# Gate rows of the attention on ScalarE's DMA queue, and another spacing of the weight-block sums

## The chip, the cores and the metric

The kernel runs on one core of one Trainium2 chip. A core has five engines that run their own instruction streams: TensorE (PE in the profile, its weight loads PEld), VectorE (DVE), ScalarE (ACT), GpSimd (POOL) and SyncE (SP). DMAs are issued from SP, ACT or POOL and are moved by 16 DMA engines that all issuers share. The metric is the device time of one execution in microseconds; lower is better.

## The reference

One layer of a streaming encoder on 512 positions of width 1024, all in float32:

```python
hn = rmsnorm(h, norm_mix_g)
fq, fk, fv, ff, gq, gf, gi, gg = split(hn @ w_in)
log_f = log_sigmoid(ff + fox_f_bias)              # 8 heads of 64
fox = softmax(q k^T / 8 + F[t] - F[s], causal) v  # F = cumsum(log_f), per head
rec = hgrn2_chunkwise(gq, gf, gi, lb)             # gated linear recurrence, 4 heads, state 128x128
rec = rmsnorm(rec, hgrn_norm_g) * silu(gg)
h += concat(fox, rec) @ w_out
h += cross_attention(rmsnorm(h), rmsnorm(mem))    # 4 heads of 256, 256 memory tokens
h += relu(rmsnorm(h) @ w1)**2 @ w2                # d_ff = 4096
out = rmsnorm(h, final_norm_g)
```

## The kernel before

All matrix products are made in a reduced float32 format, with each operand split into a high and a low part: three matmuls stand for one product. A weight block is loaded by SP into a raw buffer (`wr`), ScalarE copies it to its high part (`wh`, line 178), VectorE subtracts to get the low part (`wl`, line 182). There are two raw buffers for the blocks ahead of the MLP (`a` and `b` halves of each numbered panel: wr16b is the second half of panel 16), so the load of a block waits for the low part of the block two before it.

The order on TensorE is written out by hand; on the other engines a scheduler at build time orders instructions by priority (program order, moved by `ahead(...)`), and every engine then runs its list strictly in that order. Between steps of the recurrence and the attention, `fill.run(us)` puts in pieces of projections, so that TensorE has work while the other engines make the softmax.

The stages are: projections and the linear recurrence (to about 155 us), the forgetting attention (about 155 to 278), output projection, cross attention, then the MLP from about 447 us.

The forgetting attention runs over `pairs`: 4 pairs of heads, p, by 4 query blocks, tb; step n = 4p + tb. A step issues the scores of n (lines 996 and 997), the softmax of n (`fox_softmax`: VectorE takes the bias and the row maximum at line 1007, ScalarE the exponential at 1009, VectorE divides at 1011), the transposes of the probabilities of step n-1 (line 1019), and on POOL the bias of step n+1 (lines 987 and 988). The bias needs the row F of its head on all 128 partitions: the gate row `nF` (128x512, 256 KB), read by a broadcasting DMA from the small DRAM buffer Fd. `fox_rows(p)` (line 852) issues the two rows of a pair; for pair 0 it is called in the recurrence at chunk 2, for the later pairs at the end of step tb = 2 of the pair before. `bi`, `nF`, `pts` (the transposed probabilities) and other tiles share a pool of ten buffers.

The MLP's eight groups of hidden units are each done with seven products of half-size blocks in place of eight (groups 2 to 7 in the up half, all in the down half). For this, sums of blocks of w1 (`wsu`) and w2 (`wsd`) are made in DRAM by DMAs from POOL's queue: for each group a list of eight, four that copy a block (line 427) and four that add a block onto it (line 425, accumulating):

```python
for name, add in (("5", 0), ("7", 0), ("5", 1), ("7", 1), ("6", 0), ("6", 1), ("4", 0), ("4", 1)):
```

Two lists, one of w2 and one of w1, are taken in turn, 112 DMAs of 512 KB in all. When they go out is set by `Presum`. Each projection step reports its modelled TensorE time as credit by `presum.tick`; when the credit reaches `self.next` the next DMA is issued, held back by a dependency on the matmul that reported. PACE gives the distance to the following one by the stretch of credit. A distance of None means that no sum is issued by credit up to the next stretch; there, in the attention, each step n issues one sum by `presum.emit()` (line 1087).

```python
while self.jobs and self.spent >= self.next:
    gap = next(gap for begin, gap in reversed(PACE) if self.next >= begin)
    if gap is None:
        self.next = min(begin for begin, _ in PACE if begin > self.next)
        continue
    self.emit()
    self.next += gap
```

Of the kernel before, what the change touches and what calls it, by code (L numbers as in the profile page):

```python
# [16 lines left out]
P = 128  # L17
# [21 lines left out]
NEG = -3.0e38  # L39
SEVEN = (2, 3, 4, 5, 6, 7)  # L40
RAWS, HB, LOADS = 5, 4, 7
PACE = (25.0, 3.0), (106.0, None), (183.0, 3.1), (306.0, 7.0)


@with_exitstack
def emit(
# [22 lines left out]
    te, ve, ac, gp = nc.tensor, nc.vector, nc.scalar, nc.gpsimd  # L69
# [38 lines left out]
    def t2(name, dt=F32, shape=(S,)):  # L108
        return t2p.tile([P] + list(shape), dt, tag="t2", name=name)
# [172 lines left out]
    class Fill:  # L282
        def __init__(self):
            self.q = deque()
            self.credit = 0.0
# [143 lines left out]
    class Presum:  # L429
        def __init__(self):  # L430
            self.jobs, self.spent, self.next, self.at = deque(), 0.0, PACE[0][0], None

# [12 lines left out]
        def tick(self, us, at):  # L445
            self.spent, self.at = self.spent + us, at
# [5 lines that stand above are left out]
# [176 lines left out]
    for hp in range(2):  # L628
        wt = next_panel()
        for j in range(2):  # L630
            h = 2 * hp + j
# [64 lines left out]
    for hp in range(2):  # L696
# [8 lines left out]
        for j in range(2):  # L705
            h = 2 * hp + j
# [6 lines left out]
    Fd = drp.tile([FH, S], F32, name="Fd")  # L713
# [43 lines left out]
    for li, m in enumerate(mlev):  # L757
# [18 lines left out]
        for hp, ps in enumerate(lvs):  # L776
# [18 lines left out]
            for j in range(2):  # L795
                h = 2 * hp + j
# [53 lines left out]
    fF = {}  # L850

    def fox_rows(p):
        for h in (2 * p, 2 * p + 1):
            fF[h] = t2(f"nF{h}")
            gp.dma_start(fF[h], Fd[h, :].partition_broadcast(P))

    mt = []

# [35 lines left out]
    for c in range(NT):  # L894
# [38 lines left out]
        if c == NF:  # L933
            fox_rows(0)
# [122 lines left out]
    for n in range(len(pairs) + 2):  # L1057
# [25 lines left out]
        if n < len(pairs):  # L1083
            fox_scores(*pairs[n])
            if n + 1 < len(pairs):
                fox_biases(n + 1)
            dma = presum.emit()
            if dma is not None:
                tc.keep_in_program_order(dma)
            if tb == 2 and p < 3:  # L1090
                fox_rows(p + 1)
# [606 lines left out]
```

## Time and profile before

| | us |
|---|---|
| median of 3 runs | 764.89 (763.89 to 765.5) |
| profiled execution | 766.35 |
| its span | 764.6 |
| TensorE busy in the span | 749.8 |
| VectorE busy | 538.7 |
| ScalarE busy | 429.9 |
| POOL busy | 228.9 |

The span runs from the first to the last instruction; the profiled execution's own time has 1.75 us around it. Busy times are those of the engines' own instructions. In a timeline a line reads: start, duration, engine, source line, operation, what is written from what is read, shapes, how many were merged, and in brackets the idle time before it and what ended that.

### The profile page before, as it was taken

The page shows a single profiled execution, that of the slowest core. Times are in us where ns is not written, and L with a number is a line of the kernel's source. Part 1 is how long each engine was busy: PE and PEld are TensorE (multiplying, and loading weights), DVE is VectorE, ACT ScalarE, POOL GpSimd, SP SyncE. Part 2 cuts the span into 40 slices and gives each one's busy share as a digit, 9 for nine tenths or more (in the row PEclk, how much of TensorE's full clock was granted, in tenths as well). Part 3 has the DMA queues.
Part 4 walks back from the last instruction along what each step waited for, and adds up shares of the span by engine and source line. Part 5 has one row for each costly group of instructions (what it writes and reads, how often), then busy time and mean ns, then how long its engine had stood idle before and what let it go on. Part 6 is the DMA issues. An engine that isn't in the chain of part 4 may idle for free.

```text
span 764.6 us, 12052 instructions
## 1 busy us (share of the span) xinstructions
PE 749.8 (98%) x4501; PEld 651.7 (85%) x4501; DVE 538.7 (70%) x844; ACT 429.9 (56%) x715; POOL 228.9 (30%) x330
## 2 busy tenths in 40 slices
PE   9999999999997999999999999999999999999996
PEld 6888888888886988888888888898999999998985
DVE  5648773677876657646555558887878797969697
ACT  5654565555754543325443367557575757574773
POOL 7228554444553417841121211101011111000014
PEclk9999999999999999999999999999999999999998
DMA  8689899775878799997497959697969887947342
GB/s 248 193 239 202 194 232 213 184 167 146 214 236 191 215 227 239 228 265 166 141 187 183 260 141 259 210 305 218 307 222 262 250 267 260 272 143 257 129 138 110
DMA packets 99068, 162.86 MB, mean 213 GB/s; under 512 B 6481, under 2 KB 67450, under 8 KB 98562
## 3 DMA queue, kind: packets, MB, share of 16 engines
q0 software_dynamic: 28608, 66.61, 40.2%
q1 hardware_dynamic: 69810, 94.43, 37.5%
q10 hardware_dynamic: 592, 1.05, 0.4%
q8 instruction: 35, 0.57, 0.3%
q14 instruction: 23, 0.19, 0.1%
HBM read 157.87 MB, written 62.93 MB: 289 GB/s over the span
## 4 chain that ended last, share of the span: by engine, by line
PE 88%; DVE 4%; ACT 2%; DMA 2%; issue 2%; POOL 1%; POOLq 0%; ACTq 0%; DVEq 0%; SPq 0%
PE U L1503 4%; PE U L1504 4%; PE U L1505 4%; PE uU L1378 3%; PE uU L1377 3%; PE uU L1376 3%; PE xq L243 2%; PE wo L243 2%; PE xq L244 2%; PE xw L243 2%; PE xq L245 2%; PE xw L245 2%; PE xw L244 2%; PE wo L245 2%; PE u L245 2%; PE u L243 2%
## 5 line engine op out<-in xcount | busy, mean ns | idle before, releaser
L182 DVE TENSOR_TENSOR wld<-wrd,whd 128x1024 fp32r<-128x1024 f32 x56 | 68.5, 1224 | 20.0 <-ACT whd L178 20.0
L178 ACT ACTIVATE whd<-wrd 128x1024 fp32r<-128x1024 f32 x56 | 59.1, 1056 | 26.3 <-PE U L1505 6.5
L425 POOL DMA_DIRECT2D wsd<-in_w_dram x32 | 34.5, 1077 | 112.1 <-PE U L1505 27.4
L178 ACT ACTIVATE whu<-wru 128x1024 fp32r<-128x1024 f32 x42 | 44.4, 1056 | 36.9 <-PE uU L1377 15.4
L182 DVE TENSOR_TENSOR wlu<-wru,whu 128x1024 fp32r<-128x1024 f32 x42 | 50.4, 1222 | 13.3 <-ACT whu L178 13.3
L1503 PE MATMUL U<-whd,hb 128*128 128x512 f32 x120 | 46.8, 390 | 0.0
L1504 PE MATMUL U<-wld,hb 128*128 128x512 f32 x120 | 46.8, 390 | 0.0
L1505 PE MATMUL U<-whd,hb 128*128 128x512 f32 x120 | 46.7, 389 | 0.0
L425 POOL DMA_DIRECT2D wsu<-in_w_dram x24 | 28.5, 1188 | 50.0 <-PE xq L245 8.8
L987 POOL TENSOR_SCALAR bi<-nF,Ft 128x128 f32<-128x128 f32 (+3 forms) x32 | 21.6, 681 | 49.3 <-PE pt L1019 20.8
L1599 POOL TENSOR_TENSOR fa<-acc,gfin 128x512 f32<-128x512 f32 x4 | 6.5, 1656 | 87.6 <-DVE acc L1469 85.2
L427 POOL DMA_DIRECT2D wsd<-in_w_dram x16 | 10.9, 680 | 55.4 <-PE gq L245 13.8
L1378 PE MATMUL uU<-x_hi,wlu 128*128 128x256 f32 x96 | 27.2, 283 | 0.0
L1376 PE MATMUL uY<-xs_hi,whu 128*128 128x256 f32 x96 | 27.2, 283 | 0.0
L1377 PE MATMUL uY<-xs_lo,whu 128*128 128x256 f32 x96 | 27.2, 283 | 0.0
L1378 PE MATMUL uY<-xs_hi,wlu 128*128 128x256 f32 x96 | 27.2, 283 | 0.0
L1376 PE MATMUL uU<-xs_hi,whu 128*128 128x256 f32 x96 | 27.2, 283 | 0.0
L1377 PE MATMUL uU<-xs_lo,whu 128*128 128x256 f32 x96 | 27.2, 283 | 0.0
L1378 PE MATMUL uU<-xs_hi,wlu 128*128 128x256 f32 x96 | 27.2, 283 | 0.0
L1377 PE MATMUL uU<-x_lo,whu 128*128 128x256 f32 x96 | 27.2, 283 | 0.0
L1376 PE MATMUL uU<-x_hi,whu 128*128 128x256 f32 x96 | 27.1, 283 | 0.0
L1133 ACT ACTIVATE x_hi<-hT,gv 128x512 fp32r<-128x512 f32 x16 | 11.5, 716 | 27.5 <-DVE hT L1132 27.5
(997 smaller groups left out, 2695.7 us busy)
## 6 DMA issues: line engine op xcount, KB each, us to landing
wsd<-in_w_dram POOLq DMA_DIRECT2D x48, 512.0 KB, 7.0
wsu<-in_w_dram POOLq DMA_DIRECT2D x36, 512.0 KB, 7.3
wrd<-wsd SPq DMA_DIRECT2D x32, 512.0 KB, 6.3
wrd<-in_w_dram SPq DMA_DIRECT2D x24, 512.0 KB, 5.5
wru<-wsu SPq DMA_DIRECT2D x24, 512.0 KB, 4.5
wru<-in_w_dram SPq DMA_DIRECT2D x18, 512.0 KB, 4.9
wsd<-wsd POOLq DMA_DIRECT2D x16, 512.0 KB, 5.4
wsu<-wsu POOLq DMA_DIRECT2D x12, 512.0 KB, 4.2
```

Of the source, the lines that this page charges most:

```text
L178: ac.activation(hi, raw, AF.Copy)
L182: ve.tensor_tensor(lo, raw, f(hi), ALU.subtract)
L243: te.matmul(ps, wh, hi, start=n_ == 0 and not begun, stop=False)
L244: te.matmul(ps, wh, lo, start=False, stop=False)
L245: at = te.matmul(ps, wl, hi, start=False, stop=k == order[-1])
L425: yield gp.dma_start(dst, block(g, b), accum_op=ALU.add)
L1376: te.matmul(ps[:, i, :], whi[:, k, ws], xh[:, k, :], start=begin, stop=False, skip_group_check=True)
L1377: te.matmul(ps[:, i, :], whi[:, k, ws], xl[:, k, :], start=False, stop=False, skip_group_check=True)
L1378: at = te.matmul(ps[:, i, :], wlo[:, k, ws], xh[:, k, :], start=False, stop=k == UK - 1, skip_group_check=True)
L1503: te.matmul(ps, hi, whi[:, k, :], start=begin, stop=False, skip_group_check=True)
L1504: te.matmul(ps, hi, wlo[:, k, :], start=False, stop=False, skip_group_check=True)
L1505: at = te.matmul(ps, lo, whi[:, k, :], start=False, stop=k == 1, skip_group_check=True)
```

## The change

The two gate rows of each pair are loaded through ScalarE's DMA queue instead of POOL's, and the distances in PACE are altered: 4.0 in place of 3.0 ahead of the attention, 3.0 in place of 3.1 from credit 183, and 6.0 in place of 7.0 from 306. The number of sums per step of the attention is not touched.

```diff
-PACE = (25.0, 3.0), (106.0, None), (183.0, 3.1), (306.0, 7.0)
+PACE = (25.0, 4.0), (106.0, None), (183.0, 3.0), (306.0, 6.0)
...
     def fox_rows(p):
         for h in (2 * p, 2 * p + 1):
             fF[h] = t2(f"nF{h}")
-            gp.dma_start(fF[h], Fd[h, :].partition_broadcast(P))
+            ac.dma_start(fF[h], Fd[h, :].partition_broadcast(P))
```

## The prediction

> **What bounds the kernel now.** I read the page first, then who waited for whom on TensorE, then the timeline of all engines around each wait, and the DMA landings last.
>
> ```profile
> PE 749.8 (98%) x4501; PEld 651.7 (85%) x4501; DVE 538.7 (70%) x844; ACT 429.9 (56%) x715; POOL 228.9 (30%) x330
> ```
>
> TensorE is busy for 749.8 us of a span of 764.6. No change that leaves its matmuls alone can win more than the rest, about 15 us, and most of that is the start and the last normalisation. The waits of TensorE inside the kernel:
>
> ```profile
> PE pt L1019 <- DVE dn L1010: 4.0, 1, 4.0
> PE warm L355 <- DVE ones L359: 1.3, 1, 1.3
> PE gg L271 <- DVE z L671: 1.2, 1, 1.2
> PE pst L906 <- DVE rec L927: 1.1, 1, 1.1
> PE pt L1019 <- DVE bi L1011: 0.7, 1, 0.7
> ```
>
> One wait stands out: a transpose of attention probabilities, 4.0 us. I call the attention's sixteen steps n = 0 to 15 (head pair p = n div 4, query block n mod 4), and T(n) the transposes of step n's probabilities. This wait is ahead of T(11). In the timeline of TensorE:
>
> ```profile
> 241.51 0.28 PE L245 MATMUL xk<-meh,wl18b 128*128 128x256 f32 x1
> 245.80 0.44 PE L1019 MATMUL pt<-ident,bi 128*128 128x128 f32 x1 [4.01 <-DVE dn L1010]
> ```
>
> It costs more than its length, since the granted clock (the third column from the right, behind the engines' busy times) is halved behind it:
>
> ```profile
> 246.00:248.00 2.00, 2.00 (x11) 2.00 (x11) 1.94 (x3) 1.48 (x2) 0.99 (x1) 0.50 1.07 187
> 248.00:250.00 2.00, 2.00 (x11) 2.00 (x11) 1.56 (x9) 0.88 (x4) 2.00 (x5) 0.50 0.94 298
> 250.00:252.00 2.00, 2.00 (x13) 2.00 (x13) 0.51 (x3) 0.34 (x1) 0.52 (x1) 0.58 0.93 240
> ```
>
> Lost there: 2 x 0.50 + 2 x 0.50 + 2 x 0.42 = 2.8 us. The place is worth 4.0 + 2.8 = 6.8 us, by far the largest thing that this change can touch. Why does it wait? VectorE had the maximum of step 11 early, but ScalarE came to the exponential late:
>
> ```profile
> 237.92 0.68 DVE L1007 CUSTOM_DVE_ANT_0 bi<-ps,bi 128x512 f32<-128x512 f32 x1
> ```
>
> ```profile
> 236.18 0.47 ACT L1023 ACTIVATE pts<-pt 128x384 f32<-128x384 f32 x1
> 241.68 1.06 ACT L178 ACTIVATE wh19a<-wr19a 128x1024 fp32r<-128x1024 f32 x1 [5.02 <-DMA wr19a<-in_w_xkv_dram]
> 242.64 0.71 ACT L1009 ACTIVATE bi<-bi,mx 128x512 f32<-128x512 f32 x1
> ...
> 244.63 0.72 ACT L1009 ACTIVATE bi<-bi,mx 128x512 f32<-128x512 f32 x1 [0.71 <-DVE mx L1007]
> ```
>
> In ScalarE's order the split of the weight block wr19a stands ahead of step 11's exponentials, and it sat 5.02 us for the load. From its start (241.68) to T(11) (245.80) are 4.1 us. So the end is set by the landing of wr19a:
>
> ```profile
> 232.46 0.37 SPq L198 DMA_DIRECT2D wr19a<-in_w_xkv_dram  x1
> ```
>
> ```profile
> nF<-Fd POOLq DMA_DIRECT2D x2, 256.0 KB, 9.4
> wr19a<-in_w_xkv_dram SPq DMA_DIRECT2D x1, 512.0 KB, 9.2
> ```
>
> Issued at 232.46, landed 9.2 us later, while on POOL's queue two sums of weight blocks (accumulating, L425) and the gate rows nF of pair 3 were under way:
>
> ```profile
> 230.70 1.16 POOL L425 DMA_DIRECT2D wsu<-in_w_dram  x1
> 231.36 1.67 POOL L855 DMA_DIRECT2D nF<-Fd  x2
> 240.92 0.36 POOL L987 TENSOR_SCALAR bi<-nF,Ft 128x128 f32<-128x128 f32 x1 [7.89 <-DMA nF<-Fd]
> ```
>
> POOL itself waited 7.89 us for those rows, with the next sum queued behind the waiting bias. TensorE did not: step 12's bias was ready before TensorE came out of its own wait.
>
> **The gate rows on ScalarE's queue.** POOL loses eight issues, ScalarE gains eight. Prices, from the only transfers of this size that ScalarE issues and from the rows now:
>
> ```profile
> L1579 ACTq DMA_DIRECT2D out_dram<-fo x4: 338/364/383, 755.0 to 760.7; - x4
> ```
>
> ```profile
> L855 POOL DMA_DIRECT2D nF<-Fd x8: 548/608/1106, 146.2 to 231.9; - x8
> ```
>
> POOL is relieved of 8 x 0.61 = 4.9 us, worth nothing by itself, since none of TensorE's waits above ends on POOL. ScalarE pays 2 x 0.36 = 0.73 us per pair. An issue also waits, in ScalarE's order, for its buffer; the buffer is that of the pair before, free once POOL has made the last bias of that pair, and the exponentials and weight splits would queue behind it. Where the pairs fall, ScalarE sits idle:
>
> ```profile
> 147.07 1.06 ACT L178 ACTIVATE wh11b<-wr11b 128x1024 fp32r<-128x1024 f32 x1 [1.35 <-PE pk L244]
> ```
>
> ```profile
> 207.40 0.60 ACT L961 ACTIVATE xvh<-xv 128x512 fp32r<-128x512 f32 x1 [0.76 <-PE xv L273]
> ```
>
> 1.35 us beside pair 0's issue and 0.76 beside pair 2's, and by the 5.02 us above there is room at pair 3. I take 0, with 0.7 us as upper bound if a pair falls outside such a gap on the way to the 0.7 us wait of T(0).
>
> The transfers themselves: now nF stands behind the sum in POOL's queue, and wr19a shares the engines with one other queue. After the change nF has a queue of its own, all three run at once, and the share of wr19a shrinks until nF is through. The bound comes from the rate of the time when these transfers end:
>
> ```profile
> 237.00:241.00 4.00, 4.00 (x27) 3.61 (x26) 1.61 (x4) 0.00 (x0) 0.08 (x1) 1.00 0.98 331
> ```
>
> The pair is 2 x 256 KB, 0.52 MB, at 331 GB/s 1.6 us. At most all of it goes ahead of wr19a (+1.6 us for T(11)), at least none of it does (0). As nF and wr19a landed within a microsecond of each other (231.4 + 9.4 and 232.46 + 9.2), nearly all of nF now yields to the weight load, and I take +1.5. nF itself should land sooner than 9.4 us; nobody on the path waits for that.
>
> [...]
>
> **The spacing of the sums.** The credit (modelled TensorE time) at which sums go out is read from the code. Before: from 25 every 3.0 up to 106, 27 sums; 16 in the attention, one a step; 40 from 183 at 3.1; 29 from 307 at 7.0. After: from 25 every 4.0, 21 sums; the same 16; 41 from 183 at 3.0; 34 from 306 at 6.0. Ahead of the attention POOL issues six fewer; TensorE's two waits there, 1.2 and 1.1 us, end on VectorE behind chains through several engines. I take 0 for that, with a gain of up to 1 as bound.
>
> In the attention the number is the same, but the sequence is six sums further back. It has copies (L427, 5c 7c, 6c, 4c) and accumulating sums (L425) in turn for two groups. Before, steps 0, 3, 4, 9, 10, 11, 12 and 15 accumulate; after, 0, 1, 2, 5, 6, 9, 10 and 15. So at T(11)'s place (steps 9 and 10) nothing becomes lighter, and step 5 and 6 go from copies to accumulating sums, beside pair 2's rows. What that means, the landings at 199.9 and 204.8 (copies) against those at 225.6 and 230.7 (accumulating):
>
> ```profile
> DMA to landing us min/median/max: 4.8/5.9/6.9
> ```
>
> ```profile
> DMA to landing us min/median/max: 8.1/8.6/9.1
> ```
>
> The weight block then in flight is wr16b. Its split is ahead of step 7's exponentials, as wr19a's is ahead of step 11's:
>
> ```profile
> 203.12 0.37 SPq L198 DMA_DIRECT2D wr16b<-in_w_xkv_dram  x1
> ```
>
> ```profile
> 207.89 1.05 ACT L178 ACTIVATE wh16b<-wr16b 128x1024 fp32r<-128x1024 f32 x1
> ```
>
> ```profile
> 215.86 1.03 PE L1019 MATMUL pt<-ident,bi 128*128 128x128 f32 x8
> ```
>
> If wr16b takes as long as wr19a did, it lands at 212.3, and 4.1 us on, at 216.4, T(7) can start: 0.5 us late. At the lower end it still lands by 211.7 and costs 0. At the upper end it loses another 2.2 us, by which the slowest landing of the accumulating sums exceeds that of the copies (9.1 less 6.9): 2.7 us late. I take 0.5, from the nearest row.
>
> Behind the attention the sums are five or six places late, and denser in the MLP. First and last sum of before in that stretch, and the first fetch of stored sums for the last MLP group:
>
> ```profile
> 442.03 0.71 POOL L427 DMA_DIRECT2D wsu<-in_w_dram  x1 [2.74 <-PE u L245]
> ...
> 656.00 1.05 POOL L425 DMA_DIRECT2D wsd<-in_w_dram  x1 [6.16 <-PE U L1505]
> ```
>
> ```profile
> 683.14 5.73 SPq L1304 DMA_DIRECT2D wru<-wsu  x2
> ```
>
> Credit 307 to 503 took 214 us, 1.09 us a unit. The last sum that group 7's up half needs goes from credit 391 to 408, about 552 us, and is fetched after 683; the very last moves by one unit. No load comes ahead of its sum. Denser sums (one in 6.5 us for one in 7.6) meet a TensorE that is never idle there:
>
> ```profile
> 520.00:600.00 80.00, 80.00 (x520) 73.41 (x519) 65.29 (x80) 52.91 (x72) 9.09 (x10) 1.00 0.85 250
> ```
>
> I take 0: weight blocks are split several ahead of use, and 0.85 of the DMA time leaves room. Without that cover one late block costs what wr19a's does.
>
> **The sum.** 1.5 (T(11)) + 0.5 (T(7)) + 0 + 0 = +2.0 us. The profiled execution took 766.35, 1.75 us around its span of 764.6; it would come to 768.4. The median of the runs shown, 764.89, lies 1.46 below it; on that scale the forecast is 766.9. Its own range is 765.5 to 769.5, from the bounds above.
>
> **The rivals.** *T(11)'s wait goes (faster).* One mechanism: wr19a's split no longer holds up step 11's exponentials. It decides at a landing by 237.6 us (4.1 ahead of 241.7), or at an order on ScalarE with the exponentials first. For it: POOL's queue is rid of 0.52 MB just there, ScalarE's order is laid out anew around the new issues, and the split isn't needed by TensorE for many microseconds. Against: the same bytes are in flight at the same time, with equally heavy sums. Full price -6.8 us, 758.1; where the load is only a few microseconds earlier, 759 to 763. Chance 0.37.
>
> *Nothing on the path moves.* Rows, sums and weight loads share the engines as before, only who issues differs; 764.9, within a microsecond and a half. For it: none of TensorE's waits ends on POOL or on nF. Chance 0.13. [...]
>
> *A second wait of T(11)'s size.* The issues and the shifted sums put another block's split late ahead of exponentials, long enough to halve the clock: +6.8, 771.7. For it: 5.02 us waits for a load do occur; against: only one such in sixteen steps. Chance 0.15.
>
> **How the numbers follow.** Forecast 0.35, of it all slower; with the second wait slower is 0.50. Faster 0.37, same 0.13. A measurement here tells about 0.2% (1.5 us). Cases of both signs are nearly as likely, so the range runs from the full gain to the second wait, 758.0 to 772.0, leaving out a tenth on either side.
>
> **What would show it.** Right: T(11) still waits 4 to 6 us on wr19a's split, the clock halved behind it; nF lands in well under 9.4 us; T(7) waits up to a microsecond; accumulating sums at steps 5 and 6. Wrong: no idle time ahead of T(11), or a wait at a step not named here, or ScalarE waiting at the new issues themselves.

## The result and the profile after

The changed kernel takes 764.3 us (median of 20 executions, 761.13 to 766.92) beside 765.63 for the kernel before on the same chip (763.89 to 767.77). The ratio is 0.9981, interval 0.9972 to 0.9991. In a second measurement it was 762.9 beside 765.07, ratio 0.9969 (0.9955 to 0.9984). So it is faster by 0.2 to 0.3%, 1.3 to 2.2 us. The forecast was 766.9, slower: the time lies in the range, the sign is wrong. A ratio is formed from the executions of both kernels and need not be the quotient of their medians. Two executions are left out of the medians and ratios below as slow: one of 1244.83 us, whose granted clock was 0.557, and one of 770.91.

The profiled execution took 761.13 with a span of 759.4. It is the shortest of its 20, so its span, 5.2 us below that of before, shows the change at its best and not what it mostly does. The first row of its page and the waits of TensorE:

```profile
PE 747.1 (98%) x4501; PEld 649.1 (85%) x4501; DVE 533.4 (70%) x844; ACT 429.9 (57%) x715; POOL 227.0 (30%) x322
```

```profile
PE pt L1019 <- DVE dn L1010: 3.1, 1, 3.1
PE pst L906 <- DVE rec L927: 1.5, 1, 1.5
PE warm L355 <- DVE ones L359: 1.3, 1, 1.3
```

The rows of `gg` (1.2) and of `pt <- DVE bi` (0.7, ahead of T(0)) are gone. The wait at T(11) is still there, a microsecond shorter. TensorE's timeline has T(7) and T(11):

```profile
214.52 1.03 PE L1019 MATMUL pt<-ident,bi 128*128 128x128 f32 x8
243.50 1.22 PE L1019 MATMUL pt<-ident,bi 128*128 128x128 f32 x8 [3.05 <-DVE dn L1010]
```

T(7) has no bracket, so it waited for nothing. Behind T(11) the granted clock (third column from the right) stays at full speed, where before it was halved:

```profile
244.00:246.00 2.00, 2.00 (x19) 1.94 (x18) 1.94 (x3) 1.06 (x2) 1.65 (x2) 1.00 0.16 54
246.00:248.00 2.00, 2.00 (x19) 2.00 (x19) 1.52 (x9) 1.26 (x5) 1.36 (x4) 1.00 0.47 154
```

This adds up: 1.2 + 0.7 + (4.0 - 3.05) + 2.8 of clock, less 0.4 that `pst` waits longer, is 5.3 us of the 5.2. On ScalarE and SP around both places:

```profile
209.68 1.06 ACT L178 ACTIVATE wh16b<-wr16b 128x1024 fp32r<-128x1024 f32 x1 [2.95 <-DMA wr16b<-in_w_xkv_dram]
...
229.12 0.33 ACTq L855 DMA_DIRECT2D nF<-Fd  x1
229.83 0.33 ACTq L855 DMA_DIRECT2D nF<-Fd  x1
...
239.37 1.06 ACT L178 ACTIVATE wh19a<-wr19a 128x1024 fp32r<-128x1024 f32 x1 [4.46 <-DMA wr19a<-in_w_xkv_dram]
```

```profile
231.12 0.37 SPq L198 DMA_DIRECT2D wr19a<-in_w_xkv_dram  x1
```

```profile
nF<-Fd ACTq DMA_DIRECT2D x2, 256.0 KB, 4.9
wr19a<-in_w_xkv_dram SPq DMA_DIRECT2D x1, 512.0 KB, 8.2
```

The gate rows are issued at 229.1, 2.2 us earlier than before (231.36), and land in 4.9 us instead of 9.4. The load of wr19a is issued 1.34 us earlier, because the whole program is that far ahead, and takes 8.2 us instead of 9.2. That last microsecond is the one by which T(11) waits less. Seen from the load, the rows go out 2.0 us ahead of it, where before they went out 1.1 ahead.

### The profile page after: what moved, and what is told of

Read it like the earlier page. It is cut to its first block, busy times and chain, and to the rows that moved or that the text cites. A ratio compares the mean times of both kernels' runs of the same rounds, so it can differ in the third digit from the quotient of the medians.

```text
span 759.4 us, 12056 instructions
## 1 busy us (share of the span) xinstructions
PE 747.1 (98%) x4501; PEld 649.1 (85%) x4501; DVE 533.4 (70%) x844; ACT 429.9 (57%) x715; POOL 227.0 (30%) x322
## 4 chain that ended last, share of the span: by engine, by line
PE 95%; DMA 2%; DVE 1%; ACT 1%; issue 1%; POOL 0%; ACTq 0%; SPq 0%
PE U L1504 4%; PE U L1503 4%; PE U L1505 4%; PE uU L1378 3%; PE uU L1377 3%; PE uU L1376 3%; PE xq L243 2%; PE wo L243 2%; PE xq L244 2%; PE xq L245 2%; PE xw L245 2%; PE xw L244 2%; PE xw L243 2%; PE u L245 2%; PE wo L244 2%; PE u L244 2%
## 5 line engine op out<-in xcount | busy, mean ns | idle before, releaser
L425 POOL DMA_DIRECT2D wsd<-in_w_dram x32 | 34.7, 1084 | 104.0 <-PE uU L1378 22.1
L425 POOL DMA_DIRECT2D wsu<-in_w_dram x24 | 28.5, 1186 | 53.9 <-PE xq L245 8.7
L427 POOL DMA_DIRECT2D wsd<-in_w_dram x16 | 10.9, 680 | 56.8 <-PE gq L245 14.5
```

The source lines that it names most:

```text
L425: yield gp.dma_start(dst, block(g, b), accum_op=ALU.add)
```

## The experiments

The theory after the result: a weight block that lands late, with its split ahead of exponentials in ScalarE's order, is the only wait in the attention that counts, and the DMAs in flight beside it set how late it is. Rivals: the order on ScalarE alone is to blame; the load's own queue sets its time; the new queue, or the new spacing, is enough by itself. Every kernel was timed against the kernel before on its chip, in executions that took turns with it.

### Each part alone, and the split moved

**Queue alone.**

```diff
-            gp.dma_start(fF[h], Fd[h, :].partition_broadcast(P))
+            ac.dma_start(fF[h], Fd[h, :].partition_broadcast(P))
```

> The gate rows on ScalarE's queue, the sums spaced as before. Theory Q (the gain is the rows': wr19a lands sooner once nF has left POOL's queue, 8.2 us for 9.2): T(11) waits about 3 us for 4.0, faster by 1 us, by up to 4 where the clock is not halved. Theory S (the gain is the sums', ahead of the attention): no difference, within 1 us, and T(11) waits 4 us as before. By the prediction on record, slower by 1.5.

Measured 765.08, ratio 0.9999 (0.9987 to 1.0011): no difference. In the profile the rows land sooner, wr19a a little, T(11) waits a little less, and the waits ahead of the attention stay:

```profile
245.76 1.39 PE L1019 MATMUL pt<-ident,bi 128*128 128x128 f32 x8 [3.73 <-DVE dn L1010]
```

```profile
nF<-Fd ACTq DMA_DIRECT2D x2, 256.0 KB, 5.2
wr19a<-in_w_xkv_dram SPq DMA_DIRECT2D x1, 512.0 KB, 8.8
```

**Spacing alone.**

```diff
-PACE = (25.0, 3.0), (106.0, None), (183.0, 3.1), (306.0, 7.0)
+PACE = (25.0, 4.0), (106.0, None), (183.0, 3.0), (306.0, 6.0)
```

> The other spacing of the sums, the gate rows on POOL's queue as before. Theory Q: no difference or, by heavier sums beside pair 2's rows, slower by up to 1 us. Theory S: the waits of 1.2 us (gg) and 0.7 us (T(0)) are gone, faster by 1 to 2 us, and T(11) still waits 4 us. By the prediction on record, slower by 0.5.

Measured 765.12, ratio 0.9993 (0.9982 to 1.0005): nothing that can be told from none. In its profile the waits on `gg` and at T(0) are gone, as in the changed kernel, but T(11) waits as long as before:

```profile
243.47 1.94 PE L1019 MATMUL pt<-ident,bi 128*128 128x128 f32 x8 [4.13 <-DVE dn L1010]
```

**The split of panel 19 behind step 11's exponentials** (kernel before). `len(stream) == 20` holds for panel 19 alone, since panels count from 0.

```diff
-                ac.activation(hi, raw, AF.Copy)
+                at = ac.activation(hi, raw, AF.Copy)
+                if pin:
+                    tc.keep_in_program_order(at)
...
-                    split()
+                    split(pin=len(stream) == 20)
```

> The kernel before, with the split of weight block 19 pinned on ScalarE behind step 11's exponentials. If T(11)'s wait is only the order on ScalarE and is worth 4.0 us and the halved clock 2.8 us, it is gone and the time falls by 4 to 6.8 us. Rival: the late block 19 is wanted next, another wait takes its place, and the time falls by less than 2 us.

Measured 765.01, ratio 1.0 (0.9983 to 1.0017). T(11) waits no more, but two steps on the next late block stands ahead of T(13)'s work. From ScalarE's and TensorE's timelines (source lines are two higher here):

```profile
252.29 1.06 ACT L178 ACTIVATE wh20b<-wr20b 128x1024 fp32r<-128x1024 f32 x1 [1.92 <-DMA wr20b<-in_w_xkv_dram]
```

```profile
256.72 1.09 PE L1021 MATMUL pt<-ident,bi 128*128 128x128 f32 x4 [3.56 <-DVE bi L1013]
```

So the order at this one place is not the cause: with it changed, the next late load is passed on in the same way.

**The changed kernel again**, on this chip.

> The changed kernel once more, to see another of its executions: its times spread over 761 to 767 us and the profiled one was the shortest. Theory: the spread is T(11)'s wait being shorter or longer than what halves the clock; an execution of 763 to 766 us then shows a wait of 3.5 us or more with a clock of 0.50 behind it. Rival: the difference lies spread over the other stages and T(11) waits 3 us at full clock again.

Measured 762.9, ratio 0.9969 (0.9955 to 0.9984). Its profile, an execution of 763.6, is more typical than the first: T(11) waits 3.6 us, and the clock drops for a while (0.89 over 240 to 255 us, where the first profile has 1.00).

```profile
243.41 1.79 PE L1019 MATMUL pt<-ident,bi 128*128 128x128 f32 x8 [3.63 <-DVE dn L1010]
```

### The sums beside the late load taken away

**Two sums less, kernel before.** No sum is lost; the sequence goes on two places later.

```diff
-            dma = presum.emit()
+            dma = None if n in (9, 10) else presum.emit()
```

> The kernel before, without the sums of steps 9 and 10 (they follow later). Theory (contention: wr19a is late because two heavy sums are in flight with it): wr19a lands in 4 to 6 us after its issue instead of 8.6 to 9.2; T(11) waits under 1 us instead of 3.7 to 4.0, its clock is not lowered, the profiled span is 5 to 7 us shorter, and the median falls to 759 to 761. Rival 1 (the wait only moves to the next late block, as when panel 19's split was put behind): T(11) does not wait, but one of T(12) to T(14) does, for 2 to 4 us, and the median stays within 0.2% of 765. Rival 2 (the load's own queue sets its time): it still lands in 8 to 9 us and nothing changes.

Measured 764.51, ratio 0.999 (0.9971 to 1.0009). wr19a landed in 4.6 us and T(11)'s wait was gone, as the theory had it. But the time did not follow, as the first rival had it; the wait came back at T(15), a step later than that rival named. POOL, SP, ScalarE and TensorE, in this order:

```profile
250.19 1.06 POOL L425 DMA_DIRECT2D wsd<-in_w_dram  x1 [0.36 <-issue]
256.09 1.17 POOL L425 DMA_DIRECT2D wsu<-in_w_dram  x1
```

```profile
258.18 0.37 SPq L198 DMA_DIRECT2D wr22b<-in_w_out_dram  x1
```

```profile
266.91 1.06 ACT L178 ACTIVATE wh22b<-wr22b 128x1024 fp32r<-128x1024 f32 x1 [3.94 <-DMA wr22b<-in_w_out_dram]
```

```profile
270.44 0.63 PE L1019 MATMUL pt<-ident,bi 128*128 128x128 f32 x4 [2.60 <-DVE bi L1011]
```

Two accumulating sums (L425) at steps 13 and 14 are now beside wr22b, which is ready 8.7 us after its issue, and T(15) waits. The profiled execution took 761.1, 3.4 us less than the median, so what the slower executions do is not seen here.

**Two sums less, changed kernel.** The same edit.

> The changed kernel, without the sums of steps 9 and 10 (they follow later). Theory (contention): of the changed kernel's waits the 3.1 to 3.6 us ahead of T(11) goes; the time falls from 763 to 764 by 3 to 5 us, to 758.5 to 760.5. Rival 1 (the wait moves on): a wait of 2 to 4 us at one of T(12) to T(14), median 762 to 764. Rival 2 (the load's own queue): landing 8 us, median 762 to 764.

Measured 759.66, ratio 0.9927 (0.9903 to 0.995). Here the theory is borne out in time as well. T(11) on TensorE has no wait:

```profile
239.53 1.04 PE L1019 MATMUL pt<-ident,bi 128*128 128x128 f32 x8
```

No other wait came in the attention. 1.7 us of waits appeared in the first MLP group.

**21 sums at the old spacing** (kernel before).

```diff
-PACE = (25.0, 3.0), (106.0, None), (183.0, 3.1), (306.0, 7.0)
+PACE = (43.0, 3.0), (106.0, None), (183.0, 3.1), (306.0, 7.0)
```

> The kernel before with 21 sums ahead of the attention, as in the changed kernel, but at the old spacing of 3.0 from credit 43 on. Theory (the spacing is what takes away the waits ahead of the attention): the wait of 1.2 us on gg's chain between 75 and 100 us stays (TensorE busy 23.8 to 23.9 of 25 there), the 0.7 us ahead of T(0) may stay or go, and the median is 765 as before. Rival (the number of sums, and with it which of them fall into the attention, is what counts): both waits go as with the new spacing, and the median is that of the new spacing alone, 764.5 to 765.

Measured 765.43, ratio 1.0005 (0.9986 to 1.0023). Neither reading of the waits was right in full. TensorE's busy time (second number) shows the wait on `gg` nearly gone although the sums there are as dense as before, and the 0.7 us ahead of T(0) still there:

```profile
75.00:100.00 25.00, 24.78 (x189) 19.75 (x188) 20.40 (x50) 14.69 (x28) 18.47 (x24) 1.00 0.96 224
150.00:200.00 50.00, 49.31 (x325) 43.24 (x324) 37.41 (x91) 32.64 (x77) 22.86 (x43) 1.00 0.69 167
```

**All splits of panels 12 to 23 in program order** (changed kernel): the edit of panel 19, with `12 < len(stream) <= 24`. These reach back into the attention's first half (in the kernel before, the first of them begins at 162.0 us), further than the expectation says.

> The changed kernel, with all splits of the panels of the attention's second half kept on ScalarE in the order of their place in the program (behind the exponentials of the step). Theory (the order alone is to blame for T(11)'s wait): no wait over 1 us in the attention, profiled span 4 us shorter, median 759 to 761. Rival (the loads are late, and whichever split stands ahead of the exponentials passes it on): when panel 19 alone was put behind, the wait came back as 3.56 us at T(13); with all of them behind it comes back at the products of the late panels themselves, 1 to 4 us in 240 to 275, and the median stays within 0.3% of the changed kernel's.

Measured 775.53, ratio 1.0127 (1.0092 to 1.0163), a loss that neither reading gave in size. The splits come so late that products wait for them, and T(6) and T(7) wait too, 2.61 and 2.04 us:

```profile
209.54 1.18 PE L1021 MATMUL pt<-ident,bi 128*128 128x128 f32 x6 [2.61 <-DVE dn L1012]
...
248.15 0.39 PE L245 MATMUL xk<-meh,wh18a 128*128 128x256 f32 x1 [1.90 <-ACT wh18a L178]
```

### Which part counts once T(11) is clear

All kernels from here on leave out the sums of steps 9 and 10, unless it says otherwise.

**New spacing, rows on GpSimd's queue.**

> The new spacing, gate rows on GpSimd's queue as before, and no sums at steps 9 and 10. Theory (late weight blocks are what counts, and both spacing and the two sums bring them earlier; the queue of the gate rows matters little once the sums are gone): no wait at T(11), profiled span 758 to 759.5, median 759.5 to 761. Rival (the two parts of the change only work together: with the rows on GpSimd's queue the gain stays away, as it did for the spacing alone): median 763.5 to 765.

Measured 759.26, ratio 0.9925 (0.9911 to 0.9939): as fast as with both parts. The place where the kernel before without the two sums waited (POOL, SP, ScalarE):

```profile
249.14 0.67 POOL L427 DMA_DIRECT2D wsd<-in_w_dram  x1
254.84 0.71 POOL L427 DMA_DIRECT2D wsu<-in_w_dram  x1
```

```profile
256.27 0.37 SPq L198 DMA_DIRECT2D wr22b<-in_w_out_dram  x1
```

```profile
262.05 1.06 ACT L178 ACTIVATE wh22b<-wr22b 128x1024 fp32r<-128x1024 f32 x1 [0.39 <-DMA wr22b<-in_w_out_dram]
```

Steps 13 and 14 issue copies (L427) here, since the sequence stands six places further back, and wr22b is ready 5.8 us after its issue.

**New queue, old spacing.**

> The gate rows on ScalarE's queue, the old spacing, and no sums at steps 9 and 10. Theory (spacing counts: the old one leaves the waits of 1.2 and 0.7 us ahead of the attention, and other sums in its last steps): no wait at T(11), waits on gg's chain and at T(0) as before, median 761.5 to 764. Rival (the queue is what counts once T(11) has no wait): median 759.5 to 761.5.

Measured 763.9, ratio 0.9983 (0.996 to 1.0005), executions from 759.01 to 769.38. Steps 13 and 14 accumulate again, and T(15) waits again, with the clock at 0.50 from 274 to 276 us:

```profile
272.13 0.63 PE L1019 MATMUL pt<-ident,bi 128*128 128x128 f32 x4 [3.13 <-DVE bi L1011]
```

**One sum less** (changed kernel, step 10 only).

```diff
-            dma = presum.emit()
+            dma = None if n == 10 else presum.emit()
```

> The changed kernel without the sum of step 10 alone. Theory (the wait is as long as the bytes in flight make wr19a late): wr19a lands between 4.6 us (two sums left out) and 8.2 to 8.8 us (none), at 6 to 7; T(11) waits 0.5 to 2 us with the clock not lowered, median 760 to 762, between 759.7 and 763.5. Rival (only the sum whose transfer covers wr19a's issue counts, that of step 10, issued half a microsecond ahead of it): as with two sums left out, landing under 5 us and no wait.

Measured 764.44, ratio 0.9984 (0.996 to 1.0008). For wr19a the rival was right: it landed in 4.7 us with only the sum of step 10 gone. The time was neither's. Later blocks were late in this execution, and the same chain of split, activation and product passed it on. That sums issued ahead of wr27b and wr35b made them late is argued from the attention, not shown.

```profile
315.56 1.06 ACT L178 ACTIVATE wh27b<-wr27b 128x1024 fp32r<-128x1024 f32 x1 [3.51 <-DMA wr27b<-in_w_xq_dram]
...
437.34 1.06 ACT L178 ACTIVATE wh35b<-wr35b 128x1024 fp32r<-128x1024 f32 x1 [5.96 <-DMA wr35b<-in_w_dram]
```

```profile
320.04 0.50 PE L244 MATMUL xq<-x_lo,wh26b 128*128 128x512 f32 x1 [1.20 <-DVE x_lo L1134]
...
439.06 0.50 PE L243 MATMUL u<-x_hi,wh34b 128*128 128x512 f32 x1 [2.06 <-ACT x_hi L1133]
```

**The two sums made up for behind the attention** (changed kernel).

```diff
-PACE = (25.0, 4.0), (106.0, None), (183.0, 3.0), (306.0, 6.0)
+PACE = (25.0, 4.0), (106.0, None), (183.0, 2.8), (306.0, 6.0)
```

> The changed kernel without the sums of steps 9 and 10, which are made up for by a spacing of 2.8 for 3.0 from credit 183 on. A try at the faster version. Theory (the sums' place behind the attention costs nothing): same as with the two left out and not made up for, 759 to 760.5. Rival (the 1.7 us of waits between 480 and 500 us, in the first MLP group's second half, come from sums that are two places late): they go, 757.5 to 758.5.

Measured 761.77, ratio 0.9955 (0.9936 to 0.9975): by the medians 2 us more than without, though the intervals overlap. Neither reading gave this. The waits in the first MLP group shrank to 0.2 us, and others came at the cross attention's projection, 1.44 and 1.33 us:

```profile
319.81 0.49 PE L243 MATMUL xq<-x_hi,wh26b 128*128 128x512 f32 x1 [1.44 <-ACT x_hi L1133]
```

**New spacing behind the attention alone.**

```diff
-PACE = (25.0, 3.0), (106.0, None), (183.0, 3.1), (306.0, 7.0)
+PACE = (25.0, 3.0), (106.0, None), (183.0, 3.0), (306.0, 6.0)
```

> The kernel before without the sums of steps 9 and 10, with the new spacing behind the attention alone (3.0 and 6.0; ahead of it 3.0 as before). Theory (the gain comes from the part ahead of the attention): waits of 1.2 us on gg's chain and 0.7 us at T(0) as before, a wait at T(15) on panel 22's split, median 763.5 to 765. Rival (the gain comes from the closer sums behind): 759 to 760.5.

Measured 766.28, ratio 0.9999 (0.9978 to 1.0019): nothing. T(15) waits, and here the clock drops behind it:

```profile
270.55 1.09 PE L1019 MATMUL pt<-ident,bi 128*128 128x128 f32 x4 [2.66 <-DVE bi L1011]
```

```profile
270.00:272.00 2.00, 1.45 (x7) 1.48 (x8) 1.86 (x4) 0.71 (x2) 0.00 (x0) 0.64 0.78 264
272.00:274.00 2.00, 2.00 (x11) 1.90 (x9) 0.37 (x1) 0.00 (x0) 0.14 (x1) 0.51 0.84 250
```

**The number of sums alone**: 21 ahead of the attention at the old spacing, the new spacing behind.

```diff
-PACE = (25.0, 3.0), (106.0, None), (183.0, 3.1), (306.0, 7.0)
+PACE = (43.0, 3.0), (106.0, None), (183.0, 3.0), (306.0, 6.0)
```

> Without the sums of steps 9 and 10; ahead of the attention 21 sums as in the changed kernel, but at the old spacing of 3.0 from credit 43 on; the new spacing behind. Theory (the number counts: it sets which sums stand in the attention's steps and so which weight block is late): no wait at T(15), median 759 to 761, with the 0.7 us at T(0) perhaps left. Rival (the wider spacing counts, as it leaves DMA time to the loads ahead): 763 to 765, with a wait at T(15) or a new one in 75 to 200 us.

Measured 759.61, ratio 0.9918 (0.9896 to 0.994): the whole gain, without the wider spacing. The 0.7 us at T(0) stayed. No wait at T(15); ScalarE stood 0.16 us ahead of the split of wr22b, and for an exponential, not the load.

```profile
262.40 1.06 ACT L178 ACTIVATE wh22b<-wr22b 128x1024 fp32r<-128x1024 f32 x1 [0.16 <-ACT bi L1009]
```

**24 sums at a spacing of 3.5**, the new spacing behind.

```diff
-PACE = (25.0, 3.0), (106.0, None), (183.0, 3.1), (306.0, 7.0)
+PACE = (25.0, 3.5), (106.0, None), (183.0, 3.0), (306.0, 6.0)
```

> Without the sums of steps 9 and 10; ahead of the attention a spacing of 3.5 from credit 25 on, 24 sums; the new spacing behind. Theory (the number counts by the place of each sum): another block is late somewhere, with a wait of 2 to 4 us, median 761 to 764. Rival (less is simply better): between the 764.5 of 27 sums and the 759.3 of 21, with no wait in the attention, median 760 to 762 and waits of 0.3 to 1 us ahead of it.

Measured 766.38, ratio 1.002 (0.9996 to 1.0044): fewer sums than before, and yet nothing gained; both readings had given a shorter time. Other sums accumulate beside another block. POOL, then ScalarE:

```profile
258.08 1.09 POOL L425 DMA_DIRECT2D wsd<-in_w_dram  x1
260.30 1.17 POOL L425 DMA_DIRECT2D wsu<-in_w_dram  x1 [1.13 <-PE xk L245]
```

```profile
271.12 1.06 ACT L178 ACTIVATE wh23a<-wr23a 128x1024 fp32r<-128x1024 f32 x1 [4.95 <-DMA wr23a<-in_w_out_dram]
```

TensorE then waited 1.34 and 0.94 us for products of the attention (`pv`), with the clock at 0.96 over 255 to 300 us, and the wait on `gg` grew to 2.0 us. So fewer is not simply better. That the place of each sum in the sequence counts fits all of these runs, but no run moved one sum and left the rest where they were.

### The eight corners

Median in us and ratio to the kernel before on the same chip:

| | all sums | sums of steps 9 and 10 later |
|---|---|---|
| neither part | 765.07 | 764.51, 0.999 (0.9971 to 1.0009) |
| queue | 765.08, 0.9999 (0.9987 to 1.0011) | 763.9, 0.9983 (0.996 to 1.0005) |
| spacing | 765.12, 0.9993 (0.9982 to 1.0005) | 759.26, 0.9925 (0.9911 to 0.9939) |
| both (the change) | 762.9, 0.9969 (0.9955 to 0.9984) | 759.66, 0.9927 (0.9903 to 0.995) |

In three kernels the profile shows TensorE waiting for no late block, neither in the attention nor at the cross attention behind it: spacing, both, and the number alone, each with the two sums later. They are the fastest. Their executions, six each, lie within 1.3, 3.4 and 1.5 us, where those of the other kernels, mostly twice as many, spread over 3.5 to 10.4. They beat both kernels; the simplest of them leaves the rows on GpSimd's queue.

## Why the prediction was wrong

**The term for T(11) had the wrong sign.** The step "I take +1.5", by which a third busy queue holds wr19a up, failed: it was the author's estimate, and no run shows it. The load did not get slower: 8.2, 8.8 and 8.8 us with the rows on ScalarE's queue, 9.2, 9.3 and 9.8 with them on GpSimd's (profiles of the two kernels, of each part alone, of the repeat and of the later start; 8.6 where the split was moved). T(11) waited 3.05, 3.73 and 3.63 us against 4.01, 4.13 and 4.61. Beside the profile of before, the wait gave -1.0, -0.3 and -0.4 us in place of +1.5. The lowered clock behind it had cost 2.8 us before; it cost nothing in the first profile of the changed kernel and 15 x 0.11 = 1.7 us in the repeat (0.89 over 240 to 255 us).

Why the load did not get slower is only in part known. The prediction took all three queues to run at once, and so they did: the rows were under way from 229.1 to about 234, the load from 231.1. What it had not worked out is when ScalarE would issue the rows. They go out beside POOL's sum (229.12 and 229.83, the sum 229.35) and no longer behind it, with a lead of 2.0 us on the load (1.1 before). It also took wr19a to be the one that pays. What took longer was the sum issued with the rows: 9.5 us in the changed kernel, 9.1 before. No run changes the lead alone, so this stays an argument.

**The term for the sums ahead of the attention was too small.** The prediction gave 0 with a gain of up to 1. The waits on `gg` (1.2) and at T(0) (0.7) went in all three profiles of kernels with the new spacing and all sums. Beside the profile of before, `pst` gave back up to 0.4, which leaves 1.5 to 1.9 us, above the stated bound. But `pst` waited 1.1 us in that profile and only 0.2 to 0.7 in the five others with 27 sums ahead of the attention; beside these the gain is 0.6 to 1.5. The failed step was to put these waits down to chains of engines, and not to ask what the sums do to them. That the DMA load is their cause is not shown. Its share at 50 to 75 us fell from 0.96 to 0.71, but 21 sums at the old spacing removed the one wait and left the other, and with 24 sums the share was 0.74 and the wait on `gg` 2.0 us.

**T(7) cost nothing.** Steps 5 and 6 do accumulate, and wr16b came late enough for ScalarE to stand 2.95 us, as forecast. But its split began 7.9 us after the issue at 201.78, not 9.2, and T(7) followed 4.8 us later without a wait. The 0.5 was sized by too slow a landing.

**The range.** The forecast's own range, 765.5 to 769.5, does not follow from the bounds named: 0 to 1.6, 0 to 2.7, 0 to 0.7 and -1 to 0 add up to 763.9 to 769.9. That the time lies within 758.0 to 772.0 says nothing for the mechanism, since this range was laid to hold a full gain and a full loss. The rival in which T(11)'s wait goes needed a landing by 237.6; it came at 239.4, so the wait only got shorter.

**What was right.** ScalarE's eight new issues, 0.33 to 0.44 us each in the profile of the changed kernel, cost nothing that shows. The relief of POOL was worth nothing (0.9999 with the queue alone). The wait at T(11) does end on the landing of wr19a, and it was gone in the nine profiles in which the load landed in 4.2 to 5.0 us. The closer spacing behind the attention is worth nothing (0.9999).

**What the prediction did not see** is that a shifted sequence brings other sums beside other loads. It noted that the change moves the sequence by six places and followed this to steps 5 and 6 alone. In both kernels as they stand, steps 13 and 14 issue copies, so nothing changes at wr22b, and T(11)'s wait bounds the attention. Once the two sums beside wr19a go later, the number ahead of the attention decides what stands beside wr22b: accumulating sums with 27, copies with 21. This is worth 0.6 to 0.8% (ratios 0.9983 against 0.9927, 0.999 against 0.9925, 0.9999 against 0.9918). In the profiles T(15)'s wait of 2.6 to 3.1 us goes with it; that this is the whole of the gain is not shown.

**What stays open.** Queue alone and spacing alone gave no time that can be told from none, although their profiles have waits shorter by 0.3 us at T(11) and by 1.9 ahead of the attention; together they give 0.2 to 0.3%. The intervals allow a plain sum of small gains, and they allow that only both together bring T(11)'s wait near the 3.05 us behind which the clock stayed at 1.00 in the first profile of the changed kernel. One profile of each kernel cannot tell, and executions of one kernel differ by more than the effect.

## What to carry to other kernels

When a wait ends on a load, look first at which transfers were issued in the few microseconds ahead of it, and of what kind. Background DMAs that are issued in a fixed sequence couple distant places: a change in their number ahead of a stage changes which of them fall beside each load in it. Here 27 ahead of the attention put accumulating sums beside wr22b, which was ready 8.7 us after its issue, and 21 put copies there, 5.8 us (both with the sums of steps 9 and 10 later). So follow the shifted sequence past every load, not only past the one that waits now. A wait that is removed alone may bring nothing until the next late load is clear as well: here the ratio was 0.999 without T(11)'s wait and 0.9925 without T(15)'s too. So try such changes together, and look at the spread of the times beside the median.

## What the runs showed of the hardware

In the attention a weight load landed the later, the more of the 512 KB sums issued just ahead of it accumulate. wr23a landed in 4.5 to 5.2 us where the last two sums ahead of it were copies (five profiles: the changed kernel with two sums less, with one less and with the two made up for, the new spacing and the number alone with two less). It took 5.9 to 6.8 where one of the two accumulates (four: both kernels as they stand, the kernel before and the new queue with two sums less). With 24 sums, where both do, ScalarE stood 4.95 us for it. wr22b was ready 8.7 us after its issue behind two accumulating sums (kernel before, two sums less) and 5.8 behind two copies (new spacing, two sums less); wr19a landed in 8.2 to 9.8 us with the accumulating sum of step 10 just ahead of it (seven profiles) and in 4.2 to 5.0 without (nine). These counts leave out the kernel with panels 12 to 23 held back. Behind the attention it is less regular: wr31a took 6.2 us behind two copies (kernel before) and wr26a 6.9 behind two accumulating sums (changed kernel).

In these profiles the length of an idle time does not decide alone whether the clock drops. 3.05 us (the changed kernel) and 2.60 us (kernel before, two sums less) left it at 1.00. Behind 2.66 us (spacing behind alone) it was 0.64 and 0.51 in the two stretches of 2 us from 270 us, and behind 3.13 us (new queue, old spacing, two sums less) 0.76, 0.50 and 0.89 in the three from 272 us. What else decides it was not shown.
